# Row softmax with temperature: whole-tile scaling on VectorE, maxima in halves of a tile, and a last store in two parts

## The chip, the cores and the metric

One core of one Trainium2 chip. The time is the device time of one execution in microseconds (us). "Span" is the time from the first to the last instruction in the profiled execution; in nearly all kernels here the time is 1.8 us more than the span. Every run used in a comparison was fast (not over 1.5% above the fastest run of the same kernel), with a granted clock of 1.0. The sets of runs went to several chips; each has runs of the kernel before beside it, and its ratios are to those.

## The reference

```python
x = np.random.randn(16, 1024, 512).astype(np.float32)
x_scaled = x / 2.0
x_max = np.max(x_scaled, axis=-1, keepdims=True)
exp_x = np.exp(x_scaled - x_max)
return (exp_x / np.sum(exp_x, axis=-1, keepdims=True)).astype(np.float32)
```

33.5 MB are read and 33.5 MB written. In this text a "row" is 512 elements in each of 128 partitions, 262,144 bytes; the kernel has 128 of them.

## The kernel before

Rows travel in ten tiles of 3, 7, eight less one of 15, and 13 rows. A tile is one load and one store (the load of tile 1 alone goes in three parts). Inside a tile, VectorE and ScalarE work on chunks of 3 to 5 rows. An arena of 100 rows in SBUF holds tiles 0 to 7; the loads of tiles 8 and 9 reuse places and wait for the stores of tiles 0 to 2, and 2 and 3.

```python
PLAN = [     # chunks of each tile, place in the arena
    ([3], 0), ([4, 3], 3), ([5] * 3, 10), ([5] * 3, 25), ([5] * 3, 40), ([5] * 3, 55),
    ([5] * 3, 70), ([5] * 3, 85), ([5] * 3, 0), ([5, 4, 4], 15),
]
LAG = 2
AFTER = {8: 4, 9: 6}          # ScalarE issues load 8 behind its work on tile 4, load 9 behind tile 6
FUSED = {1, 2, 3}

    def do_mul(k):            # VectorE, chunk k, runs behind the maximum of chunk k + 2
        t, b, c, a = chunks[k]
        nc.vector.reciprocal(
            out=recip[:, b : b + c], in_=sums[:, b : b + c]
        )._wait_ge(s_exp, k + 1).then_inc(s_rec, 1)
        if t in FUSED:        # one instruction for the chunk
            nc.vector.tensor_mul(
                out=arena[:, a : a + c],
                in0=arena[:, a : a + c],
                in1=recip[:, b : b + c].unsqueeze(2).to_broadcast([P, c, D]),
            )._wait_ge(s_rec, k + 1).then_inc(s_mul, 1)
            return
        for r in range(c):    # one instruction for each row
            ins = nc.vector.tensor_scalar_mul(
                out=arena[:, a + r],
                in0=arena[:, a + r],
                scalar1=recip[:, b + r : b + r + 1],
            )
            # ... cut: the first waits for s_rec
        ins.then_inc(s_mul, 1)

        # ... cut: ScalarE does exp and the row sums, one instruction for each row
        for k in range(len(chunks) + LAG):
            if k < len(chunks):
                do_max(k)
            if k >= LAG:
                do_mul(k - LAG)
        for t in range(len(tiles)):        # stores, from the Sync queue
            nc.sync.wait_ge(s_mul, last_chunk[t] + 1)
            nc.sync.dma_start(out=dram(of, t), in_=sb(t)).then_inc(...)   # cut
```

## Time and profile before

| | before |
|---|---|
| time, median of 3 | 161.53 us |
| span | 159.9 us |
| both DMA queues, share of the 16 engines' span | 50.1% + 48.1% |
| VectorE (DVE) busy | 131.6 us, 82% |
| ScalarE (ACT) busy | 94.4 us, 59% |

The overview of this kernel (busy times, forty slices, DMA queues) is shown in the prediction. It is read in this way: an engine at 82% is hardly the bound if another resource is at 98%, and here that is the 16 DMA engines, which loads and stores share. So the question for any change to VectorE is not how much work it saves, but whether the DMA engines ever run out of work, and once the last load has landed (127 us) that means whether the queue of stores runs dry.

The costliest groups of VectorE's instructions by form (columns: line, engine, operation, output<-input by name, by shape, count, then busy us and mean ns of one, then idle time before them):

```profile
L105 DVE TENSOR_REDUCE negmax<-arena 128x5 f32<-128x2560 f32 x22 | 61.9, 2813 | 4.6 <-DMA arena<-in_x_dram 4.6
L125 DVE TENSOR_SCALAR arena<-arena,recip 128x512 f32<-128x512 f32 x91 | 37.8, 482 | 0.7
L118 DVE TENSOR_TENSOR arena<-arena,recip 128x2560 f32<-128x2560 f32 x6 | 16.9, 2825 | 0.2
```

Ninety-one rows are scaled one by one, thirty-seven in fused form. The stores of the last three tiles, from the Sync queue's timeline (SPq: issued at, us of the issuing itself) and the DMA view of the same stretches (last number: us from issue to landing, the transfer's last completion signal in the trace):

```profile
121.37 0.33 SPq L166 DMA_DIRECT2D out_dram<-arena  x1
out_dram<-arena SPq DMA_DIRECT2D x1, 3840.0 KB, 20.6
136.78 0.33 SPq L166 DMA_DIRECT2D out_dram<-arena  x1
out_dram<-arena SPq DMA_DIRECT2D x1, 3840.0 KB, 14.3
144.77 0.33 SPq L166 DMA_DIRECT2D out_dram<-arena  x1
out_dram<-arena SPq DMA_DIRECT2D x1, 3328.0 KB, 14.2
```

### The profile page before, as it was taken

How to read it: one execution, taken by the hardware profiler on the slowest of the kernel's cores; microseconds unless marked ns; L12 is line 12 of the kernel's file. 1: busy time of each engine (PE TensorE's matmuls, PEld its weight loads, DVE VectorE, ACT ScalarE, POOL GpSimd, SP SyncE). 2: the span in 40 equal slices, each digit the busy share in tenths (PEclk: the TensorE clock that was granted, in tenths of full speed). 3: DMA queues.
4: the chain of work that ended last, by engine and by line, in shares of the span. 5: the costliest groups of instructions: out<-in, count | busy, mean ns of one | idle time of the engine just before them, and what ended most of it. 6: DMA issues, size and time to landing. Idle time of an engine off the chain costs nothing.

```text
span 159.9 us, 476 instructions
## 1 busy us (share of the span) xinstructions
DVE 131.6 (82%) x153; ACT 94.4 (59%) x257; POOL 0.2 (0%) x4
## 2 busy tenths in 40 slices
DVE  0376499999999999999999999999999799992000
ACT  0369176768448547766688666786667948650000
POOL 0000000000000000000000000000000000000000
DMA  7998999999998989899999999998999998989993
GB/s 278 466 396 377 447 424 407 446 475 376 418 484 377 484 377 484 377 484 407 448 423 446 423 438 453 402 461 387 452 448 438 396 484 377 484 384 476 431 426 133
DMA packets 3028, 67.13 MB, mean 420 GB/s; under 512 B 337, under 2 KB 337, under 8 KB 721
## 3 DMA queue, kind: packets, MB, share of 16 engines
q1 hardware_dynamic: 1584, 34.34, 50.1%
q10 hardware_dynamic: 1440, 32.77, 48.1%
q14 instruction: 4, 0.02, 0.0%
HBM read 33.55 MB, written 33.55 MB: 420 GB/s over the span
## 4 chain that ended last, share of the span: by engine, by line
DVE 58%; DMA 31%; issue 0%; DVEq 0%; ACT 0%
DMA arena<-in_x_dram 31%; DVE negmax L105 30%; DVE arena L125 13%; DVE arena L118 13%; DVE recip L114 1%; DVEq L218 0%; ACT arena L144 0%
## 5 line engine op out<-in xcount | busy, mean ns | idle before, releaser
L144 ACT ACTIVATE arena<-arena,negmax 128x512 f32<-128x512 f32 x128 | 90.7, 710 | 42.5 <-DVE negmax L105 42.5
L105 DVE TENSOR_REDUCE negmax<-arena 128x5 f32<-128x2560 f32 (+2 forms) x27 | 72.1, 2675 | 12.2 <-DMA arena<-in_x_dram 12.2
L125 DVE TENSOR_SCALAR arena<-arena,recip 128x512 f32<-128x512 f32 x91 | 37.8, 482 | 0.7
L144 ACT ACTIVATION_READ_ACCUMULATOR arena<-arena,negmax 128x1 f32 x128 | 23.9, 187 | 0.0
L118 DVE TENSOR_TENSOR arena<-arena,recip 128x2560 f32<-128x2560 f32 (+2 forms) x8 | 21.0, 2625 | 0.3
L114 DVE RECIPROCAL recip<-sums 128x5 f32<-128x5 f32 (+2 forms) x27 | 4.8, 176 | 0.0
L144 ACT ACT_TABLE_LOAD x1 | 1.3, 1283 | 5.0 <-issue 5.0
L207 POOL MEMSET const-bfloat16-1.0<- 128x1 bf16 x1 | 0.1, 103 | 0.0
L207 POOL MEMSET const-uint8-127<- 128x1 uint8 x1 | 0.1, 103 | 0.0
L207 POOL MEMSET const-float32-1.0<- 128x1 f32 x1 | 0.1, 100 | 0.0
L207 POOL MEMSET const-float32-0.0<- 128x1 f32 x1 | 0.1, 99 | 0.2 <-issue 0.2
## 6 DMA issues: line engine op xcount, KB each, us to landing
arena<-in_x_dram ACTq DMA_DIRECT2D x7, 3840.0 KB, 42.9
out_dram<-arena SPq DMA_DIRECT2D x7, 3840.0 KB, 24.0
arena<-in_x_dram ACTq DMA_DIRECT2D x1, 3328.0 KB, 32.7
out_dram<-arena SPq DMA_DIRECT2D x1, 3328.0 KB, 14.2
out_dram<-arena SPq DMA_DIRECT2D x1, 1792.0 KB, 17.0
arena<-in_x_dram ACTq DMA_DIRECT2D x1, 1536.0 KB
arena<-in_x_dram SPq DMA_DIRECT2D x1, 768.0 KB, 6.7
out_dram<-arena SPq DMA_DIRECT2D x1, 768.0 KB, 15.5
```

The costliest lines, as they stand in the source:

```text
L105: nc.vector.reduce_max(out=negmax[:, b : b + c], in_=arena[:, a : a + c], axis=mybir.AxisListType.X, negate=True,)._wait_ge(ld[t], 48 if t ...
L114: nc.vector.reciprocal(out=recip[:, b : b + c], in_=sums[:, b : b + c])._wait_ge(s_exp, k + 1).then_inc(s_rec, 1)
L118: nc.vector.tensor_mul(out=arena[:, a : a + c], in0=arena[:, a : a + c], in1=recip[:, b : b + c].unsqueeze(2).to_broadcast([P, c, D]),)._w ...
L125: ins = nc.vector.tensor_scalar_mul(out=arena[:, a + r], in0=arena[:, a + r], scalar1=recip[:, b + r : b + r + 1],)
L144: ins = nc.scalar.activation(out=arena[:, a + r], in_=arena[:, a + r], func=mybir.ActivationFunctionType.Exp, bias=negmax[:, b + r : b + r ...
L207: nc = _bacc.Bacc("TRN2", target_bir_lowering=False, num_devices=1)
```

## The change

The intent is fewer and larger instructions on VectorE: one reciprocal and one fused multiply for a whole tile, two maxima a tile instead of three, 42 instructions instead of 153. The last tile, whose store nothing can hide, is multiplied and stored in two parts, 9 and 4 rows. The diff, cut to its core (the constants that it repeats, and FUSED, have no effect):

```diff
 PLAN = [
-    ([3], 0), ([4, 3], 3), ([5] * 3, 10), ([5] * 3, 25), ([5] * 3, 40), ([5] * 3, 55),
-    ([5] * 3, 70), ([5] * 3, 85), ([5] * 3, 0), ([5, 4, 4], 15),
+    ([3], [3], 0), ([4, 3], [7], 3), ([8, 7], [15], 10), ([8, 7], [15], 25),
+    ([8, 7], [15], 40), ([8, 7], [15], 55), ([8, 7], [15], 70), ([8, 7], [15], 85),
+    ([8, 7], [15], 0), ([5, 4, 4], [9, 4], 15),
 ]
-    def do_mul(k):
-        t, b, c, a = chunks[k]
+    def do_mul(j):
+        t, b, c, a, k = groups[j]       # a group ends with chunk k - 1
         nc.vector.reciprocal(
             out=recip[:, b : b + c], in_=sums[:, b : b + c]
-        )._wait_ge(s_exp, k + 1).then_inc(s_rec, 1)
-        if t in FUSED:
...      (cut: the form row by row goes, the fused form stays)
         for k in range(len(chunks) + LAG):
             if k < len(chunks):
                 do_max(k)
-            if k >= LAG:
-                do_mul(k - LAG)
+            while j < len(groups) and groups[j][4] + LAG <= k + 1:
+                do_mul(j)
+                j += 1
-        for t in range(len(tiles)):
-            nc.sync.wait_ge(s_mul, last_chunk[t] + 1)
-            nc.sync.dma_start(out=dram(of, t), in_=sb(t)).then_inc(
+        for j, (t, b, c, a, _) in enumerate(groups):
+            o = b - tiles[t][0]
+            nc.sync.wait_ge(s_mul, j + 1)
+            nc.sync.dma_start(out=dram(of, t)[:, o : o + c], in_=arena[:, a : a + c]).then_inc(
```

More of the change, by code (lines that the diff above doesn't have):

```diff
@@ L11 @@
 PLAN = [
-    ([3], 0), ([4, 3], 3), ([5] * 3, 10), ([5] * 3, 25), ([5] * 3, 40), ([5] * 3, 55),
-    ([5] * 3, 70), ([5] * 3, 85), ([5] * 3, 0), ([5, 4, 4], 15),
[3 rows of a table added]
 ]
 ARENA = 100
+SPREAD = 1
 LAG = 2
+FIRST = 1
+AFTER = {8: 4, 9: 6}
 SPREAD = 1
+LAG = 2
+FIRST = 1
 AFTER = {8: 4, 9: 6}
@@ L39 @@
     n_rows = N // P
-    assert sum(sum(c) for c, _ in PLAN) == n_rows
+    assert sum(sum(c) for c, _, _ in PLAN) == n_rows
     arena = nc.alloc_sbuf_tensor("arena", (P, ARENA, D), fp32)
@@ L45 @@
     recip = nc.alloc_sbuf_tensor("recip", (P, n_rows), fp32)
-    tiles, chunks, base = [], [], 0
-    for t, (cs, at) in enumerate(PLAN):
+    tiles, chunks, groups, base = [], [], [], 0
+    for t, (cs, gs, at) in enumerate(PLAN):
         r = sum(cs)
@@ L56 @@
             o += c
+        o, k = 0, len(chunks) - len(cs)
+        for g in gs:
+            first = o
+            while o < first + g:
+                o += chunks[k][2]
+                k += 1
+            assert o == first + g
+            groups.append((t, base + first, g, at + first, k))
         base += r
@@ L90, in issue_loads @@
                 continue
-            if t == 0:
-                nc.sync.dma_start(out=sb(t), in_=dram(xf, t)).then_inc(ld[t], 16)
-            elif t == SPREAD:
+            queue = nc.sync if t < FIRST else nc.scalar
+            if t == SPREAD:
                 r = tiles[t][1] - 1
-                for p, q, lo, hi in ((0, P, 0, r), (0, 126, r, r + 1), (126, P, r, r + 1)):
-                    nc.scalar.dma_start(
-                        out=sb(t)[p:q, lo:hi], in_=dram(xf, t)[p:q, lo:hi]
-                    ).then_inc(ld[t], 16)
-            else:
-                nc.scalar.dma_start(out=sb(t), in_=dram(xf, t)).then_inc(ld[t], 16)
+                parts = (0, P, 0, r), (0, 126, r, r + 1), (126, P, r, r + 1)
+            else:
+                parts = ((0, P, 0, tiles[t][1]),)
+            for p, q, lo, hi in parts:
+                queue.dma_start(
+                    out=sb(t)[p:q, lo:hi], in_=dram(xf, t)[p:q, lo:hi]
+                ).then_inc(ld[t], 16)
     def do_max(k):
@@ L110, in do_max @@
         )._wait_ge(ld[t], 48 if t == SPREAD else 16).then_inc(s_max, 1)
-    def do_mul(k):
-        t, b, c, a = chunks[k]
+    def do_mul(j):
+        t, b, c, a, k = groups[j]
         nc.vector.reciprocal(
             out=recip[:, b : b + c], in_=sums[:, b : b + c]
-        )._wait_ge(s_exp, k + 1).then_inc(s_rec, 1)
-        if t in FUSED:
-            nc.vector.tensor_mul(
-                out=arena[:, a : a + c],
-                in0=arena[:, a : a + c],
-                in1=recip[:, b : b + c].unsqueeze(2).to_broadcast([P, c, D]),
-            )._wait_ge(s_rec, k + 1).then_inc(s_mul, 1)
-            return
-        for r in range(c):
-            ins = nc.vector.tensor_scalar_mul(
-                out=arena[:, a + r],
-                in0=arena[:, a + r],
-                scalar1=recip[:, b + r : b + r + 1],
-            )
-            if r == 0:
-                ins._wait_ge(s_rec, k + 1)
-        ins.then_inc(s_mul, 1)
+        )._wait_ge(s_exp, k).then_inc(s_rec, 1)
+        nc.vector.tensor_mul(
+            out=arena[:, a : a + c],
+            in0=arena[:, a : a + c],
+            in1=recip[:, b : b + c].unsqueeze(2).to_broadcast([P, c, D]),
+        )._wait_ge(s_rec, j + 1).then_inc(s_mul, 1)
     def compute_and_store():
@@ L140, in compute_and_store @@
                 for v in behind[u]:
-                    nc.scalar.wait_ge(st[v], 16)
+                    nc.scalar.wait_ge(st[v], 16 * len(PLAN[v][1]))
                 nc.scalar.dma_start(out=sb(u), in_=dram(xf, u)).then_inc(ld[u], 16)
@@ L154, in compute_and_store @@
             ins.then_inc(s_exp, 1)
+        j = 0
         for k in range(len(chunks) + LAG):
@@ L159, in compute_and_store @@
                 do_max(k)
-            if k >= LAG:
-                do_mul(k - LAG)
-        for t in range(len(tiles)):
-            nc.sync.wait_ge(s_mul, last_chunk[t] + 1)
-            nc.sync.dma_start(out=dram(of, t), in_=sb(t)).then_inc(
+            while j < len(groups) and groups[j][4] + LAG <= k + 1:
+                do_mul(j)
+                j += 1
+        ends = 0
+        for j, (t, b, c, a, _) in enumerate(groups):
+            o = b - tiles[t][0]
+            nc.sync.wait_ge(s_mul, j + 1)
+            nc.sync.dma_start(out=dram(of, t)[:, o : o + c], in_=arena[:, a : a + c]).then_inc(
                 st[t] if t in awaited else s_end, 16
             )
-        nc.gpsimd.wait_ge(s_end, 16 * (len(tiles) - len(awaited)))
+            ends += t not in awaited
+        nc.gpsimd.wait_ge(s_end, 16 * ends)
     hook = nc.inst_callbacks[-1]
```

## The prediction

> **What bounds the kernel now.** Unit: a "row" is 512 fp32 in each of 128 partitions, 262,144 bytes. The kernel loads 128 rows and stores 128 rows, in ten tiles (3, 7, eight less one of 15, the last of 13). I read the overview first.
>
> ```profile
> span 159.9 us, 476 instructions
> DVE 131.6 (82%) x153; ACT 94.4 (59%) x257; POOL 0.2 (0%) x4
> DVE  0376499999999999999999999999999799992000
> DMA  7998999999998989899999999998999998989993
> q1 hardware_dynamic: 1584, 34.34, 50.1%
> q10 hardware_dynamic: 1440, 32.77, 48.1%
> ```
>
> The two DMA queues (stores on q1, loads on q10) fill 98.2% of the 16 engines' time. VectorE has 82%. So the DMA engines are the bound; the view by windows gives them 433 GB/s over 24 to 141 us and 435 over 60 to 156, so a row costs 262,144 / 433,000 = 0.605 us, and 256 rows 155 us. There is almost nothing to win: the span less 155 us is start, last receipt and end. The time can only grow, if the DMA engines ever have nothing to do.
>
> The chain of waits says something else, VectorE 58%, because VectorE waits for nothing but loads. I take that as "VectorE is the runner-up", and ask where the two meet. The lines of VectorE's timeline that matter:
>
> ```profile
> 18.26 2.82 DVE L105 TENSOR_REDUCE negmax<-arena 128x5 f32<-128x2560 f32 x1 [3.53 <-DMA arena<-in_x_dram]
> ...
> 30.74 0.18 DVE L114 RECIPROCAL recip<-sums 128x5 f32<-128x5 f32 x1
> 30.95 2.82 DVE L118 TENSOR_TENSOR arena<-arena,recip 128x2560 f32<-128x2560 f32 x1
> 33.69 2.81 DVE L105 TENSOR_REDUCE negmax<-arena 128x5 f32<-128x2560 f32 x1
> ...
> 127.34 2.82 DVE L105 TENSOR_REDUCE negmax<-arena 128x5 f32<-128x2560 f32 x1 [1.06 <-DMA arena<-in_x_dram]
> 130.08 0.18 DVE L114 RECIPROCAL recip<-sums 128x5 f32<-128x5 f32 x1
> 130.29 2.07 DVE L125 TENSOR_SCALAR arena<-arena,recip 128x512 f32<-128x512 f32 x5
> 132.28 2.28 DVE L105 TENSOR_REDUCE negmax<-arena 128x4 f32<-128x2048 f32 x1
> ```
>
> From start to next start: a maximum over 2560 elements 2.73 us, over 2048 2.19; reciprocal 0.21; a fused multiply over 2560 2.74, over 2048 (elsewhere) 2.21; five single-row multiplies 1.99, 0.398 a row. Between 18.26 and 126 VectorE never stops.
>
> From the view of DMA issues, asked stretch by stretch, the stores (issued, landed): tile 6 106.6, 133.0; tile 7 121.4, 142.0; tile 8 136.8, 151.1; tile 9 144.8, 159.0. Each store is issued well before the one in front of it has landed: the store queue never runs dry. Spare before tile 8's store: 142.0 - 136.8 = 5.2 us. That is the number that the change eats.
>
> **What the Trainium skill says.** "VectorE: DVE Perf Modes", the perf-mode tier table: fp32 tensor_scalar in SBUF runs at 2x, fp32 tensor_tensor and tensor_reduce at 1x. The trace agrees: 0.398 us a row against 2.74 / 5 = 0.548. "Vector Engine (DVE) Microarchitecture Reference", section 5.2: 1.0417 ns a column plus about 75 ns an instruction. The trace agrees: 2560 x 1.0417 = 2667, plus 73 is the 2.74 above; the maximum has 63. "DMA: Bandwidth & Descriptors", Anatomy of one DMA: about 2 us a DMA that don't scale with bytes, mostly the receipt. The trace agrees: the first load is issued at 0 and bytes start at 1.0 us; at the end bytes stop by 157 to 158 and the store lands at 159.0. Same page, on issuing engines: all queues share the same 16 engines; here the rate is 433 with loads and without.
>
> **The change part by part.** Every multiply becomes the fused 1x form: 91 rows lose the 0.398 form for 0.533 (512 x 1.0417 ns), 91 x 0.135 = +12.3 us; one instruction per tile instead of per chunk saves 16 reciprocals (27 to 11) of 0.2 = -3.2 us; 7 fewer maxima (27 to 20) save 7 x 0.06 = 0.4. Net some **+8.7 us** of VectorE time. ScalarE's instructions are the same 128, and loads and stores the same bytes; the repeated constants in the diff do nothing.
>
> It also moves work. The order of instructions of the changed kernel on VectorE: both maxima of tile t+1, then reciprocal and multiply of the whole tile t. The last tile: maxima of 5 and 4 rows, multiply of tile 8 (15 rows), maximum of 4, multiply of 9 rows, multiply of 4.
>
> Durations, estimates from the rows above at 1.0417 ns an element: maximum of 8 rows 4267 + 60 = 4.33 us, of 7 3.79; reciprocal of 15 columns 0.27 (0.166, 0.171, 0.178 for 3, 4, 5 in the groups: some 0.006 a column); multiply of 15 rows 8000 + 75 = 8.07, of 7 3.81, of 9 4.87, of 4 2.21. A 15-row tile: 4.33 + 3.79 + 0.27 + 8.07 = **16.46 us**. Before: 3 x 5.69 = 17.06 for tiles 2 and 3, 3 x 4.93 = 14.79 for the rest. The DMA engines need 30 x 0.605 = 18.2 us a tile, both ways: VectorE stays faster, but by less.
>
> Walk. Tile 2's maximum starts at 18.26, released by its load as now. Multiply of tile 1 ends at 18.26 + 8.12 + 0.22 + 3.81 = 30.4. Then one tile each 16.46: tile 2 at 46.9, 3 at 63.3, 4 at 79.8, 5 at 96.3, 6 at 112.7, 7 at 129.2. Maxima of the last tile 2.73 + 2.19: 134.1. Multiply of tile 8: 134.1 + 0.27 + 8.07 = **142.5**, its store issued some 0.1 later, 142.6, against 136.8 now. Then 2.19 + 0.24 + 4.87: nine rows at 149.8; + 0.20 + 2.21: four rows at 152.3.
>
> Do loads hold that up? Landings now: tile 3 29.1, 8 110.3, 9 127.3; needed at 30.4, 112.7, 129.2. The stores start a little later, so loads are no later. No wait, with 1.3 us to spare. ScalarE needs about 0.70 us a row, 10.7 a tile, inside 16.5.
>
> Now the DMA engines. Up to the landing of tile 7's store they carry the same 228 rows, with one queue or the other filled (tile 7's store is issued at 129.3, tile 6's lands at about 133): so it lands at **142.0** as now. Tile 8's store comes at 142.6. Bytes of the old one stop about 1.0 before it lands, 141.0; those of the new start 1.0 after issue, 143.6: **2.6 us of idle DMA** that were not there. Then 28 rows x 0.605 = 16.9 without a break (nine rows are issued at 149.9, before tile 8 is through at 143.6 + 9.1 = 152.7; four at 152.4, before 158.1): 160.5, plus 1.0 of receipt: 161.5, against 159.0 now. Sum **+2.5 us**; 161.5 + 2.5 = **164.0 us**, 1.6% slower.
>
> The split of the last store is worth keeping: as one store of 13 rows it would be issued at 152.4, its bytes at 153.4, 0.7 us after tile 8's were through.
>
> **Rivals.** (1) The delay stays hidden and the time is the same, 161.5: for it speak the 98% busy DMA engines, and 5.2 us of spare. Against it the walk, which eats 5.8; but a release 2 us earlier than I reckon would leave under 1 us. (2) VectorE becomes the bound outright and its end sets the time: its end moves from 144.7 to 152.3, and with 2.4 us of bytes for the last four rows and 2 of fixed cost that is only 156.7; it would need the DMA idle earlier. It would happen if a load came late: tile 3, 8 and 9 have 1 to 2.4 us to spare, and every microsecond of wait comes on top, 165 to 166. (3) Fewer instructions win time (153 to 43): against it, VectorE is not the bound and the fused form costs more a row. 160 at best, since 256 rows of DMA don't shrink.
>
> **Range and chances.** The step that carries it is the difference of two times near 142, each good to about 0.7 us; the fixed cost at the restart may differ by 0.5. 164.0, range 162.4 to 165.5. Slower by over 2% means above 164.8, 0.8 from my centre: 0.24. Faster by over 2% would need 158.3, below what the bytes allow: 0.01. Same 0.75.
>
> **What would show it.** Groups: 11 fused multiplies, 15 rows at about 8.16 us busy, no single-row multiplies; VectorE busy 140 to 143. Stores of tiles 7 and 8 issued near 129.3 and 142.6, tile 7's landing near 142. Slices of DMA: one dip of 2 to 3 us at 141 to 144, none before. No wait of VectorE for tile 9. If the dip is absent, rival 1 holds; if VectorE waits for a load after 20 us, rival 2; if the long multiply is not linear in its size, all times of the walk shift by tiles.

## The result

The changed kernel takes 163.88 us (163.77 to 163.94, 4 runs); the kernel before 161.59 us (161.50 to 161.83, 4 runs, the three above among them). The ratio is 1.0138, with a 95% interval of 1.0121 to 1.0156: slower by 1.4%, clear of the noise. Here and below, a ratio compares the fast runs of the two kernels; it is not quite the ratio of the medians quoted.

The overview of the changed kernel, to be held against the one in the prediction:

```profile
span 162.1 us, 366 instructions
DVE 141.3 (87%) x42; ACT 92.8 (57%) x257; POOL 0.2 (0%) x4
DVE  0377499999999999999999999999999999999500
DMA  7999999999999999899999989999998999588996
```

VectorE is 9.7 us busier with 111 fewer instructions. The row of DMA slices had no digit below 8 between its second and its thirty-ninth slice; now it has one 5, in the slice from 138 to 142 us. VectorE's groups, by form:

```profile
L136 DVE TENSOR_TENSOR arena<-arena,recip 128x7680 f32<-128x7680 f32 x7 | 57.1, 8158 | 0.2
L124 DVE TENSOR_REDUCE negmax<-arena 128x8 f32<-128x4096 f32 x7 | 30.9, 4413 | 3.0 <-DMA arena<-in_x_dram 3.0
L124 DVE TENSOR_REDUCE negmax<-arena 128x7 f32<-128x3584 f32 x7 | 27.1, 3876 | 0.0
```

The multiply of a tile is 8.16 us in one piece, and until it ends no row of the tile can be stored. VectorE's timeline in the stretch that matters (start, us, and so on):

```profile
121.18 8.16 DVE L136 TENSOR_TENSOR arena<-arena,recip 128x7680 f32<-128x7680 f32 x1
129.25 5.00 DVE L124 TENSOR_REDUCE negmax<-arena 128x5 f32<-128x2560 f32 x2
134.18 0.24 DVE L133 RECIPROCAL recip<-sums 128x15 f32<-128x15 f32 x1
134.45 8.16 DVE L136 TENSOR_TENSOR arena<-arena,recip 128x7680 f32<-128x7680 f32 x1
```

The two multiplies, of tiles 7 and 8, release the stores at 129.36 and 142.64:

```profile
129.36 0.33 SPq L178 DMA_DIRECT2D out_dram<-arena  x1
out_dram<-arena SPq DMA_DIRECT2D x1, 3840.0 KB, 12.6
142.64 0.33 SPq L178 DMA_DIRECT2D out_dram<-arena  x1
out_dram<-arena SPq DMA_DIRECT2D x1, 3840.0 KB, 10.5
149.94 0.33 SPq L178 DMA_DIRECT2D out_dram<-arena  x1
out_dram<-arena SPq DMA_DIRECT2D x1, 2304.0 KB, 8.7
152.36 0.33 SPq L178 DMA_DIRECT2D out_dram<-arena  x1
out_dram<-arena SPq DMA_DIRECT2D x1, 1024.0 KB, 8.8
```

Tile 7 lands at 129.36 + 12.6 = 142.0, just as before (121.37 + 20.6 = 142.0), although it was issued 8 us later: the DMA engines had other work meanwhile. Tile 8 is issued after that and finds the engines idle. The view by windows, for the changed kernel (window, its length, busy time of DVE, ACT and POOL, clock, DMA share, GB/s):

```profile
140.00:141.00 1.00, 1.00 (x1) 0.00 (x0) 0.00 (x0) 1.00 0.08 31
141.00:142.00 1.00, 1.00 (x1) 0.00 (x0) 0.00 (x0) 1.00 0.00 0
142.00:143.00 1.00, 1.00 (x2) 0.00 (x0) 0.00 (x0) 1.00 0.00 0
143.40:143.60 0.20, 0.20 (x1) 0.00 (x0) 0.00 (x0) 1.00 5.36 2304
```

A packet is what one DMA engine moves at a time, here one partition's share of a store: 30,720 bytes for 15 rows. This view books a packet's bytes where the packet starts, which is why a fifth of a microsecond can show 2304 GB/s. The trace also holds the start and the duration of each packet (1.14 us for this size). By these, 15 of the 16 engines end their last packet of tile 7 between 140.5 and 141.0 us, and one, which lags, at 141.55; the first packets of tile 8 start between 143.46 and 143.62. So all engines stand still together for 1.9 us, and one engine for 2.8 us on average. The same window of the kernel before:

```profile
141.00:142.00 1.00, 0.96 (x4) 0.92 (x4) 0.00 (x0) 1.00 1.00 430
```

### The profile page after: what moved, and what is told of

The parts are those of the page before. It is cut to its first block, busy times and chain, and to the rows that moved or that the text cites. A ratio compares the mean times of both kernels' runs of the same rounds, so it can differ in the third digit from the quotient of the medians.

```text
span 162.1 us, 366 instructions
## 1 busy us (share of the span) xinstructions
DVE 141.3 (87%) x42; ACT 92.8 (57%) x257; POOL 0.2 (0%) x4
## 4 chain that ended last, share of the span: by engine, by line
DVE 83%; DMA 10%; issue 0%
DVE arena L136 42%; DVE negmax L124 40%; DMA arena<-in_x_dram 10%; DVE recip L133 1%
## 5 line engine op out<-in xcount | busy, mean ns | idle before, releaser
L124 DVE TENSOR_REDUCE negmax<-arena 128x8 f32<-128x4096 f32 (+4 forms) x20 | 70.4, 3558 | 10.7 <-DMA arena<-in_x_dram 10.7
L136 DVE TENSOR_TENSOR arena<-arena,recip 128x7680 f32<-128x7680 f32 (+4 forms) x11 | 70.0, 6364 | 0.4
L133 DVE RECIPROCAL recip<-sums 128x15 f32<-128x15 f32 (+4 forms) x11 | 2.4, 220 | 0.0
```

What stands on the lines that cost most here:

```text
L124: nc.vector.reduce_max(out=negmax[:, b : b + c], in_=arena[:, a : a + c], axis=mybir.AxisListType.X, negate=True,)._wait_ge(ld[t], 48 if t ...
L133: nc.vector.reciprocal(out=recip[:, b : b + c], in_=sums[:, b : b + c])._wait_ge(s_exp, k).then_inc(s_rec, 1)
L136: nc.vector.tensor_mul(out=arena[:, a : a + c], in0=arena[:, a : a + c], in1=recip[:, b : b + c].unsqueeze(2).to_broadcast([P, c, D]),)._w ...
```

## The experiments

Three theories were held against each other. **D**: the DMA engines are the bound, and the change loses the time in which they are idle before tile 8's store. **V**: VectorE is the bound; the chain of waits of the changed kernel puts 83% of the span on it. **S**: smaller stores at the end cost DMA time by themselves. Each run below has its ratio to the kernel before.

### Tile 8 in halves

```diff
-    ([8, 7], [15], 0), ([5, 4, 4], [9, 4], 15),
+    ([8, 7], [8, 7], 0), ([5, 4, 4], [9, 4], 15),
```

> Tile 8's multiply and store in two pieces (8 and 7 rows), all else as changed. Theory D (the time comes from the idle DMA engines at 141 to 143.6 us, since tile 8's store is issued too late): its first piece is issued at 129.3 + 2.7 + 0.2 + 4.3 + 0.1 = 136.6, before tile 7's store is through, so the dip at 141 goes; but the nine rows of the last tile come at 150.2, their bytes at 151.2, after tile 8's end at 141.0 + 9.1 = 150.1, so a smaller gap of about 1.1 us is left: 162.6 us, between the kernels. Theory V (VectorE, 83% of the chain of waits, sets the time): VectorE's work grows by one reciprocal and one start, 0.3 us: 164.2. Theory S (small stores cost DMA time): more stores, slower than 163.9.

Measured: 162.35 us (162.21 to 162.37), ratio 1.0046. VectorE works as much as in the changed kernel (141.5 us busy) and the time falls by 1.5 us. The gap at 141 is gone, and the smaller one that D foresaw is there, with a single packet starting in the second window:

```profile
141.00:142.00 1.00, 1.00 (x1) 0.83 (x4) 0.00 (x0) 1.00 1.07 459
150.00:151.00 1.00, 0.96 (x3) 0.00 (x0) 0.00 (x0) 1.00 0.03 14
```

### Tile 8 in halves and the last tile in three

```diff
-    ([8, 7], [15], 0), ([5, 4, 4], [9, 4], 15),
+    ([8, 7], [8, 7], 0), ([5, 4, 4], [5, 4, 4], 15),
```

> As e1, and the last tile multiplied and stored in three pieces (5, 4, 4). Theory D: pieces issued at about 148.0, 150.4, 152.8, each before the bytes in front of it are through (150.1, 153.1, 155.6): no gap anywhere, 161.5 us or a little less, as the kernel before. Theory V: VectorE ends at 152.7 instead of 152.3, so 164.3. Theory S: slower than e1.

Measured: 161.71 us, ratio 1.001 (0.9996 to 1.0023). The whole loss is gone, with VectorE as busy as in any of these kernels (141.7 us) and with five stores for the last two tiles. V and S both fall here. The second window again:

```profile
150.00:151.00 1.00, 0.97 (x3) 0.00 (x0) 0.00 (x0) 1.00 1.00 424
```

### The kernel before, with tile 8 held back

The kernel before has none of the change. One, two or three maxima whose result nobody uses are put in front of the last multiply of tile 8:

```diff
+        if t == 8 and k == last_chunk[8]:      # cut: spare, 15 columns, is allocated above
+            for i in range(n):        # n = 1, 2, 3
+                nc.vector.reduce_max(
+                    out=spare[:, 5 * i : 5 * i + 5],
+                    in_=arena[:, tiles[8][2] : tiles[8][2] + 5],
+                    axis=mybir.AxisListType.X,
+                )
```

> The kernel before, with one maximum over 5 rows (2.73 us, result unused) put in front of the last multiply of tile 8, so that tile 8's store comes 2.7 us later (139.5) and so does VectorE's end (147.5). Theory D: bytes start at 140.5, before tile 7's are through at 141.0: no change, 161.6 us. Theory V: +2.7, 164.3.

> As d1 with two such maxima, 5.4 us: tile 8's store at 142.2, bytes at 143.2, 2.2 us after tile 7's. Theory D: 161.6 + 2.2 = 163.8 us, close to the changed kernel, from a kernel that has none of its changes. Theory V: +5.4, 167.0. Rival that the DMA engines hide it all: 161.6.

> As d1 with three, 8.1 us: tile 8's store at 144.9, bytes at 145.9, 4.9 us after tile 7's. Theory D: 166.5 us; from d2 to d3 every microsecond of delay counts in full. Theory V: +8.1, 169.7.

| kernel | store of tile 8 issued, us | later than before | time, us (median) | ratio | loss, us |
|---|---|---|---|---|---|
| before | 136.78 | | 161.67 | | |
| n = 1 | 139.31 | 2.5 | 161.61 | 1.0002 | 0 |
| n = 2 | 142.09 | 5.3 | 163.26 | 1.0096 | 1.6 |
| n = 3 | 144.82 | 8.0 | 165.89 | 1.0264 | 4.2 |

With n = 3 nothing starts on the DMA engines for four microseconds; one of the empty windows:

```profile
143.00:144.00 1.00, 1.00 (x4) 0.00 (x0) 0.00 (x0) 1.00 0.00 0
```

The first delay is free, which V can't explain: VectorE's end moved by 2.5 us as well. From the second to the third, 2.7 us of delay cost 2.6. For n = 2 and 3 D had said 163.8 and 166.5, 0.5 to 0.6 too much: it had reckoned with 3.2 us of free delay. Delay less loss is 5.3 - 1.6 = 3.7 and 8.0 - 4.2 = 3.8: so much delay is free in this kernel. The changed kernel fits the same line: 142.64 - 136.78 = 5.9 us late, 2.3 lost, 3.6 free.

The packets of the traces show where the rest of the free delay comes from. In the kernel before, the 16 engines end their last packets unevenly, between 157.5 and 158.55 us, and the last to end counts. After a pause all start afresh together and end within 0.2 us of each other (160.6 to 160.8 in the changed kernel). So the last byte comes later by less than the mean idle time of an engine: by 1.6, 2.2 and 4.3 us for 2.2, 2.8 and 4.9 us of idle time (n = 2, the changed kernel, n = 3), 0.6 less each time.

### Rows scaled one by one, all else as changed

```diff
-        nc.vector.tensor_mul(
-            out=arena[:, a : a + c],
-            in0=arena[:, a : a + c],
-            in1=recip[:, b : b + c].unsqueeze(2).to_broadcast([P, c, D]),
-        )._wait_ge(s_rec, j + 1).then_inc(s_mul, 1)
+        for r in range(c):
+            ins = nc.vector.tensor_scalar_mul(
+                out=arena[:, a + r],
+                in0=arena[:, a + r],
+                scalar1=recip[:, b + r : b + r + 1],
+            )
+            if r == 0:
+                ins._wait_ge(s_rec, j + 1)
+        ins.then_inc(s_mul, 1)
```

> The changed kernel with its whole-tile multiply replaced by 15 single-row multiplies (0.398 us a row instead of 0.538); groups, order and stores as changed. Theory D: VectorE gets ahead and waits for loads; the last tile's load lands at about 127.3 as before, then 4.9 of maxima, 0.3, 6.0 of multiplies: tile 8's store is issued at 138.6 and no gap opens: 161.4 us. That would lay the loss on the slower form of the multiply and not on the whole-tile grouping. A rival (grouping alone loses it): 163.9 as changed. Theory V: VectorE works 12 us less than changed, and the time falls by as much as loads allow, to 161 or below.

Measured: 161.53 us, ratio 0.9999 (0.9986 to 1.0012). Whole-tile groups, maxima in halves and the split store cost nothing when the multiply takes the quicker form. VectorE then works 18 us less than in the changed kernel (123.3 us busy), and it does not help below 161.5: it waits for loads.

```profile
128.45 5.01 DVE L124 TENSOR_REDUCE negmax<-arena 128x5 f32<-128x2560 f32 x2 [2.62 <-DMA arena<-in_x_dram]
133.38 0.24 DVE L133 RECIPROCAL recip<-sums 128x15 f32<-128x15 f32 x1
133.65 6.03 DVE L137 TENSOR_SCALAR arena<-arena,recip 128x512 f32<-128x512 f32 x15
```

Fifteen single-row multiplies take 6.0 us, the fused one 8.2. Tile 8's store is issued at 139.71 and queues behind tile 7's, which lands at 142.0. D had said 138.6 and was 1.1 us early, since the last load came that much later than before. What the larger groups save (16 reciprocals of 0.2 us, about 3 us) is small beside what the slower form of the multiply adds (12.3 us by the prediction's working).

### Rows one by one up to tile 7, whole tiles fused for 8 and 9

The edit is the one above, for tiles below 8 alone (`if t < 8:`).

> Single-row multiplies for tiles 0 to 7, the whole-tile multiply for tiles 8 and 9 alone. VectorE is ahead by tile 7 and waits for the last tile's load, which landed at 128.4 in the run with all single rows; then 4.9 of maxima, 0.3 and the fused 8.1: tile 8's store at 141.8, 0.8 us sooner than in the changed kernel (142.6), 2.1 later than with all single rows (139.7). Theory D: 163.1 us, so two thirds of the loss come from one instruction, tile 8's multiply. Rival (the loss grows with VectorE's total work, spread over all tiles): two of ten tiles carry the slow form, so about a fifth of the loss, 162.0 us.

Measured: 163.09 us, ratio 1.0087. The store of tile 8 was issued at 141.88. So 1.5 of the 2.3 us come from the form of the multiply in the last two tiles, of which only tile 8's stands in front of the late store. The other 0.8 are what tiles 2 to 7 add, because with them in fused form VectorE begins the last tile at 129.25 us and not at 128.49, when its load lets it.

### Maxima in thirds again

```diff
-    ([8, 7], [15], at)
+    ([5] * 3, [15], at)        # in all seven tiles of 15 rows
```

> The changed kernel with maxima in thirds of a tile (5, 5, 5) as before; whole-tile multiplies and split last store as changed. Theory D: a tile costs VectorE 3 x 2.73 + 0.27 + 8.07 = 16.53 us instead of 16.46, and tile 8's store still follows two maxima of the last tile: issued at about 142.9, so 164.1 us, as changed within 0.3. Rival (halves of a tile cost or win something of their own): off by over 0.5.

Measured: 164.63 us, ratio 1.0189. The store of tile 8 was issued at 142.97, as reckoned (142.9), and the span is 162.4 us, 0.3 over the changed kernel, as reckoned too. But the time is 0.75 over it, more than the 0.5 that was to speak for the rival: in all four runs of this kernel it lies 2.2 us over the span instead of 1.8. What those 0.4 us outside the span are, no run here tells. Inside the span, halves or thirds make no difference beyond the count of instructions.

### ScalarE's new wait taken away

In the changed kernel ScalarE stands idle for 7.4 us at 62 to 69, which it didn't before. The line of it in the view of waits of the changed kernel (who waited for whom, us, times, longest):

```profile
ACT arena L152 <- DMA out_dram<-arena: 7.4, 1, 7.4
```

It has come to the point in its program where it issues tile 8's load, and that waits for tile 2's store. The edit moves this point back by one tile:

```diff
-AFTER = {8: 4, 9: 6}
+AFTER = {8: 5, 9: 6}
```

> The changed kernel with tile 8's load issued one tile later in ScalarE's order, so that ScalarE no longer stands for 7.4 us at 62 to 69 on the store of tile 2 (it waits there only to issue that load). Theory D: that wait was off the path, the load queue still has loads in front of it: 163.9 us, same. Rival (that new wait costs time): faster by some tenths or more. If the load were then late: slower, with a wait of VectorE for tile 8.

Measured: 163.93 us, ratio 1.015. The wait is gone from the view and the time is the same. It was a new wait, and a long one, and off the path.

### The last store whole

In the first run, multiply and store of the last tile are one piece of 13 rows; in the second, only the store.

```diff
# first
-    ([8, 7], [15], 0), ([5, 4, 4], [9, 4], 15),
+    ([8, 7], [15], 0), ([5, 4, 4], [13], 15),
# second: in the loop of stores
+            if t == 9 and o == 0:
+                continue
+            if t == 9:
+                o, c, a = 0, tiles[t][1], tiles[t][2]
```

> The last tile multiplied and stored whole (13 rows), all else as changed. Theory D: it is issued at 152.1, its bytes start at 153.1, some 0.4 after tile 8's (152.7), and 13 rows take 7.9 us: about 164.4 us, 0.5 more than the changed kernel. Theory V: VectorE ends a little sooner (152.1) but 9 more rows follow it, +5 us: 168. Theory S: faster than 163.9, by up to 0.5.

> The changed kernel with the last tile still multiplied in two pieces (9 and 4 rows), but stored whole. The run with one multiply and one store mixed two things: there the one multiply waited 3.0 us for ScalarE's last four rows. Here only the store changes: issued at 152.4, bytes at 153.4, some 0.7 us after tile 8's are through at 152.7; 13 rows 7.9 us. Theory D: 0.7 to 1.0 us over the changed kernel, 164.6 to 164.9 us, as the prediction reckoned for one store. Theory S (small stores cost): 163.9 or less.

The first took 167.1 to 168.5 us in its three fast runs, ratio 1.0374 (a fourth run, 170.7 us, counts as slow and is left out): 3 us more than I had said, and by its number it would have pleased V. Its trace shows what I had left out:

```profile
143.76 2.28 DVE L124 TENSOR_REDUCE negmax<-arena 128x4 f32<-128x2048 f32 x1
149.03 0.24 DVE L133 RECIPROCAL recip<-sums 128x13 f32<-128x13 f32 x1 [2.99 <-ACT arena L152]
149.31 7.09 DVE L136 TENSOR_TENSOR arena<-arena,recip 128x6656 f32<-128x6656 f32 x1
```

One multiply for all 13 rows has to wait 3.0 us for ScalarE's last four, then 7 us pass before any row of the tile can leave, and the store is issued at 156.42. My expectation had forgotten ScalarE. In this execution one of the 16 DMA engines also lagged (the windows from 141 to 144 us show 31 GB/s, one packet each) and the last load came 1.0 us late; why is open. It is the run of 168.5 us; of the two other fast runs, 167.1 and 167.3, no trace was kept. The second run takes the store alone: 164.34 us, ratio 1.0167, 0.5 us over the changed kernel. The store was issued at 152.25, tile 8 had landed at 153.0. So the split of the store is worth 0.5 us here, and the split of the multiply that goes with it some 3 more (2.8 to 3.0 by the two untraced runs).

### The split store alone, in the kernel before

```diff
+            parts = [(0, tiles[t][1], last_chunk[t])]
+            if t == 9:
+                parts = [(0, 9, last_chunk[t] - 1), (9, 13, last_chunk[t])]
```

> The kernel before with one part of the change alone: the last tile stored in two parts (9 and 4 rows). Theory D: the store queue is never dry there, so at most the last engines finish more evenly: 161.3 to 161.6 us. Theory S: slower by some tenths.

Measured: 161.65 us, ratio 0.9999 (0.9986 to 1.0011). Where stores always queue, cutting the last one wins nothing and loses nothing. S has no support in any run.

No version beat the kernel before. That fits D: as long as the stores are released early enough to keep the DMA engines filled, the work for VectorE can vary from 123 to 142 us without a change in the time.

## Why the prediction was right

| step | predicted | measured |
|---|---|---|
| VectorE busy | 140 to 143 us (8.7 more) | 141.3 (9.7 more) |
| multiply of 15 rows | 8.16 us busy | 8.158 |
| a 15-row tile on VectorE | 16.46 us | 16.47 (46.89, 63.36, 79.84 ...) |
| waits for loads after the first 20 us | none | none |
| tile 7: store issued, landed | 129.3, 142.0 | 129.36, 142.0 |
| tile 8: store issued | 142.6 | 142.64 |
| first bytes of it | 143.6 | 143.5 |
| idle DMA | 2.6 us | 1.9 for all engines at once, 2.8 for one on average |
| last byte | 160.5 | 160.78 |
| last landing | 161.5 | 152.36 + 8.8 = 161.2 |
| time | 164.0 | 163.88 |

The mechanism, bytes in full supply until 141 and then a pause before tile 8's store, is the one that the trace shows, and the runs confirm it from both sides: taking the pause away by an earlier release gives the time back (tile 8 and the last tile in finer pieces), and making such a pause in the kernel before loses it (the held-back tile 8).

The path was right and some terms were off.

**The receipt.** I had added 1.0 us from the last bytes to the landing, read off the end of the kernel before, where the view shows bytes until 157 to 158 and a landing at 159.0. But the view books a packet where it starts; the last one, of 13 rows, ran 0.98 us, to 158.55. So some 0.4 us are left for the receipt, and not 1.0 (0.4 at the end of the changed kernel too, 160.78 to 161.2). Against that, the bytes of the last 28 rows took 17.3 us and not 16.9. The two errors have opposite signs and leave the 0.3 us between the predicted and the measured landing; that it is so little is partly luck. So is the 141.0 for the end of tile 7's bytes: the landing less 1.0 is close to the time when most engines are done (140.5 to 141.0) only because one engine lags to 141.55.

**The spare.** I called 142.0 - 136.8 = 5.2 us "the number that the change eats". The held-back runs show that 3.7 are free. Landing minus issue overstates it, because the engines have finished their bytes before the landing and a new store needs about 0.9 us before its own begin; my walk allowed for both, the sentence did not. Nor does it hold the 0.6 us from the uneven end of the kernel before. Put together, with 140.8 as the mean end of tile 7's bytes in the runs with a pause: 140.8 - 0.9 - 136.8 + 0.6 = 3.7.

**ScalarE at 62 us.** That it would stand for 7.4 us on the store of tile 2 was nowhere in the prediction; it did no harm.

**Small slips.** The sum of the parts gave 8.7 us more for VectorE, and 9.7 were measured; it counts 43 instructions, and there are 42. And that each store is issued before the one in front has landed holds for the four stores listed, not for all: tile 2's was issued at 45.2 us, when tile 1's had landed at 45.1, and there loads filled the engines.

**The fixed cost.** For it the prediction cites from the Trainium skill the section Anatomy of one DMA of "DMA: Bandwidth & Descriptors". That section is about DMAs which GpSimd issues; here SyncE and ScalarE issue them, and instead of 2 us the traces show 1.2 to 1.4 us for a store into idle engines: 0.8 to 1.0 before the first bytes, 0.4 after the last.

The remark that a single last store would come 0.7 us too late held for the store alone (0.5 us). As one store behind one multiply it would have been some 3 us worse, which the prediction did not see. Rival 1 (the delay stays hidden) is what happens with up to 3.7 us of delay. Rival 2 (VectorE's end sets the time) did not come about: that end moved from 144.7 to 152.3 us, by 7.6, and the time by 2.3. Rival 3 (fewer instructions win) was refuted by the busy time, which rose, and by the time.

## What to carry to other kernels

If the DMA engines are full, ask of every change to a compute engine when each store is released, and compare the release with the moment at which the bytes in front of it run out; busy shares and the chain of waits don't tell that. A larger instruction holds everything back until its end: near the end of the kernel work in small pieces, and count instructions only where their fixed cost is large beside their work. Before fusing, look at the rate: one fused multiply of 15 rows took 8.2 us where fifteen small ones took 6.0.

## What the Trainium skill lacked or had wrong

- "DMA: Bandwidth & Descriptors", Specifications: it gives a first-byte latency of about 0.6 us for the hardware path, and does not say from which moment. Here the first packets start 1.0 us after the start of the first load's issue, and 0.8 to 1.0 after that of a store's into idle engines (issued 142.64, packets from 143.46 to 143.62; issued 144.82, packets from 145.65 to 145.80). The issuing itself lasts 0.33 to 0.38 us of this, so that from its end the 0.6 is about right.
- The same page, Anatomy of one DMA: 2.0 us plus bytes over 436 GB/s makes an estimated 11.0 us for 3840 KB, with most of the 2.0 in the receipt. The page fits this on DMAs that GpSimd issues; for the Sync queue it has no such fit. Seven kernels here show 10.5 for such a store from the Sync queue into idle engines, with 0.4 for the receipt.
- No page that I used says how late a store may be released before it costs time on full DMA engines. Here it is 3.6 to 3.8 us after the release of the kernel before, 1.4 to 1.6 less than the landing of the store in front suggests.
